# Second layer with the sample rows ahead of the prompt rows, and the last head's attention units in another order

## The chip, the cores and the metric

The kernel is one program on one NeuronCore of a Trainium2 chip. The core has five engines with instruction streams of their own, coupled by semaphores: TensorE (PE; the loading of its weights is listed as PEld), VectorE (DVE), ScalarE (ACT), GpSimd (POOL) and SyncE (SP, which here issues nearly all DMAs). Each engine works through its stream in the written order. The metric is the device time of one execution in microseconds; less is better. Three executions of the kernel before took 957.39 (median), 952.74 and 958.02 us.

## The reference

One inference step of a small hybrid decoder, for a prompt of 512 rows and for 8 x 4 = 32 sample rows that share all weights, with 1024 features:

```python
# layer 1: Mamba-2 mixer (32 heads of 64, state 128, causal convolution of width 4)
hp = hp + ssd_mixer(hp, ...);  hs = hs + ssd_mixer(hs, ...)
# shared keys and values, from the rows after layer 1
kv_p = rmsnorm(hp, kv_norm) @ w_kv;  kv_s = rmsnorm(hs, kv_norm) @ w_kv
# layer 2: three dilated windows per head (distances 0, d, .., 128 d with d = 1, 4, 16), 8 heads of 128
u = rmsnorm(h, g_norm) @ w_in          # 3 x 1024 columns of q, 1024 of the gate
o_g, lse_g = attend(q_g, bias_g)       # prompt: its own keys; samples: 1024 cached keys and the new ones
o = sum_g softmax_g(lse_g) * o_g
h = h + (o * silu(gate)) @ w_out
y = rmsnorm(h, final_norm)
```

Outputs are the normed rows, the Mamba states, the convolution's last rows and the new keys and values, each for prompt and samples.

## The kernel before

All activations lie transposed, features on the 128 partitions and the T = 544 rows along the free axis. Each fp32 operand of a large product is split into a high and a low fp32r part, and three matmuls (high x high, high x low, low x high) make one product. A row half of the second layer has TH = 272 columns.

**Stages.** From 0 to about 370 us the Mamba layer runs, then its output projection (`h1_tile`, which also puts the prompt rows into an order by residue mod 4), then keys and values (`v_out`, `k_out`), and from about 590 us the second layer. In the second layer the columns of every tile are the 512 prompt rows and then the 32 samples.

**The second layer** is a list `units` with work for one head each: `attend(h, n)` is query block n (128 rows) of the prompt for head h, `sample(h, q)` is four of the eight samples, and `combine()`, once, puts the samples' three windows together with a softmax over their logsumexps. At turn u a unit begins (scores on PE, softmax on DVE and ACT); at turns u+2, u+3 and u+4 it goes on (transposes `ptp` or `w`, the product with the values `pv` or `so`, a last transpose `op`). A head's `sample` fetches its cached keys `kc` (two tiles, two buffers) and values `vc` by DMA from SP.

**The filler.** After each turn, `run(24)` (from turn 44 on, `run(20)`) issues that many matmuls of a generator `filler()`: first 16 pairs of weight tiles for q and gate, each pair as 7 products of 12 matmuls over half the rows (`pa<-bq,whi`, `pb<-bq,wlo`, ...), then `out_proj`. The pairs' results are taken from PSUM by `q_evac` and `gate_evac`; in the last pair (gates of heads 4 and 6) the seven products come in the order 0, 1, 2, 3, 4, 6, 5, where 4 and 6 share one PSUM bank `pb`, so that 6 can start only after DVE has read what 4 left there. `out_proj` makes the output projection in two parts: first columns 272 to 543, then columns 0 to 271, 8 tiles of 24 matmuls each (`pa<-yh,wo`, `pa<-yl,wo`; the last two of each part read the weights from `whi` and `wlo`). Its operand is y = attention x gate, split into `yh` and `yl` by `y_split` (L1214 on ACT, L1215 on DVE) head by head, and for the samples by `sample_y`, which needs `combine`'s result `oc` and the samples' gates `u_s`.

**At the seam** between filler and output projection `combine` itself issues 16 filler matmuls between its 16 small matmuls `oc` (128 x 16); `ahead` takes these off an earlier turn. `combine` has two more transposes on PE: `lp` (the logsumexps) and, after a softmax in small steps on DVE and ACT (L1368 to L1385), `lp2` (its weights; a row of the profile shows both as `lp`). The second call of `sample_y` stands at the very end of the last pair.

**Order.** A framework turns this into one stream per engine; ACT, DVE and SP take their instructions strictly in it, so an instruction that waits holds all behind it. `tc.high_priority()` moves some evacuations forward.

Of the kernel before, what the change touches and what calls it, by code (L numbers as in the profile page):

```python
# [15 lines left out]
ALU = mybir.AluOpType  # L16
AX = mybir.AxisListType

D = 1024
SEQ = 512  # L20
NB = 8
TS = 4
T = SEQ + NB * TS
HA = 256
HB = T - HA
# [30 lines left out]
TH = T // 2  # L56
PE_ = SEQ - TH

# [66 lines left out]
def tile_yoco_step(  # L125
# [718 lines left out]
    def h1_tile(m, pa, pb):  # L844
        xk = wk.tile([128, T], F32, name="xk", bufs=2)
        dma(xk, xT[:, m, :])
        hm = h1[m // 4][:, m % 4, :]
        nc.vector.tensor_tensor(blk(hm[:, 0:HA], 2), perm(pa[:, 0:HA], 2), perm(rs_v[:, 0:HA], 2), op=ALU.mult)
        nc.vector.tensor_tensor(blk(hm[:, HA:SEQ], 2), perm(pb[:, 0:SEQ - HA], 2), perm(rs_v[:, HA:SEQ], 2), op=ALU.mult)
        nc.vector.tensor_tensor(hm[:, SEQ:T], pb[:, SEQ - HA:HB], rs_v[:, SEQ:T], op=ALU.mult)  # L850
        nc.vector.tensor_tensor(blk(hm[:, 0:SEQ], 4), blk(hm[:, 0:SEQ], 4), perm(xk[:, 0:SEQ], 4), op=ALU.add)
        nc.vector.tensor_tensor(hm[:, SEQ:T], hm[:, SEQ:T], xk[:, SEQ:T], op=ALU.add)
# [97 lines left out]
    def v_out(h, pa, pb):  # L950
        vt = wk.tile([128, T], F32, name="vt", tag="vt", bufs=2)
        nc.vector.tensor_tensor(vt[:, 0:HA], pa[:, 0:HA], rs_h[:, 0:HA], op=ALU.mult)
        nc.vector.tensor_tensor(vt[:, HA:T], pb[:, 0:HB], rs_h[:, HA:T], op=ALU.mult)
        dma(kvT[:, 8 + h, :], vt)
        yield
        vp = pss("vp", (128, 4, 128))
        vsp = pss("vsp")
        for n in range(4):
            transpose(vp[:, n, :], vt[:, 128 * n:128 * n + 128], ident)
        transpose(vsp[0:32, 0:128], vt[:, SEQ:T], ident)  # L960
# [116 lines left out]
    def q_evac(t, half_, p, other=None, sign=1.0):  # L1077
        h, g = t
        if t not in qp_t:
            qp_t[t] = wk.tile([128, SEQ], F32, name="qp", bufs=7)  # L1080
        n = PE_ if half_ else TH
        qs = qpad[h % 3][:, :, TS * g:TS * g + TS]
        for o, c0, c1 in ((qp_t[t][:, TH * half_:TH * half_ + n], 0, n), (qs, n, TH))[0:1 + half_]:
            src = p[:, c0:c1]
            if c0:
# [5 lines left out]
            nc.vector.scalar_tensor_tensor(o, src, sign * scale, samples(add) if c0 else add, op0=ALU.mult, op1=ALU.add)  # L1091

    def gate_evac(t, half_, p, other=None, sign=1.0):
# [8 lines left out]
        nc.scalar.activation(th, c, AF.Tanh, scale=0.5)  # L1102
        n = PE_ if half_ else TH
        yt = y_t[h // 4][:, h % 4, TH * half_:TH * half_ + n]
        u = yt if h == 7 else th[:, 0:n]
        nc.vector.scalar_tensor_tensor(u, th[:, 0:n], 1.0, c[:, 0:n], op0=ALU.add, op1=ALU.mult)
# [6 lines left out]
        nc.vector.scalar_tensor_tensor(yt, yt, 0.5, u, op0=ALU.mult, op1=ALU.mult)  # L1113
        y_split(h, TH * half_, TH * half_ + n)

# [125 lines left out]
    def attend(h, n):  # L1241
# [3 lines left out]
        vb, vr = (kv[:, i, 0:SEQ].rearrange("p (n d) -> p n d", n=4) for i in (1, 2))  # L1245
        ktr = kt[:, 0:SEQ].rearrange("p (n r i) -> p r n i", n=4, r=4)
        bt12 = bt[:, 256:512].rearrange("p (a c) -> p a c", a=2)
# [8 lines left out]
        mm(sp[:, 0:g0], qp[0][:, 128 * n:128 * n + 128], kt[:, k0:128 * n + 128], start=True, stop=True)  # L1256
        s_ = wk.tile([128, 512], F32, name="s", bufs=3)
# [36 lines left out]
        yt = y_t[h // 4][:, h % 4, :]  # L1294
        if h == 7 and op_n[h] % 2 == 0:
            c0 = HA if n > 1 else 0
            assert len(gated) == 2
            nc.vector.scalar_tensor_tensor(yt[:, c0:c0 + HA], op[:, c0:c0 + HA], 0.5, yt[:, c0:c0 + HA], op0=ALU.mult, op1=ALU.mult)
            y_split(h, c0, c0 + HA)
        elif h < 7 and op_n[h] == 4:  # L1300
            nc.vector.tensor_copy(yt[:, 0:SEQ], op)
            att_done.add(h)
# [5 lines left out]
    def sample(h, q):  # L1308
# [10 lines left out]
        for o, c0, c1 in ((s1, 0, 512), (s2, 512, NU), (s2, NU, SK)):  # L1319
            for j in range(4):  # L1320
                b = 4 * q + j
                keys = kc[j // 2][:, j % 2, c0:c1] if c1 <= NU else kt[:, SEQ + TS * b:SEQ + TS * b + TS]
                mm(o[32 * j:32 * j + 32, c0 % 512:c0 % 512 + c1 - c0], qs[:, b, :], keys, start=True, stop=True)
# [79 lines left out]
    def sample_y():  # L1403
        if len(late_smp) == 1:
            nc.vector.scalar_tensor_tensor(y_s, y_s, 0.5, u_s, op0=ALU.mult, op1=ALU.mult)
# [166 lines left out]
def _unpack(r):  # L1572
    yt = r["yT"].transpose(2, 1, 0).reshape(T, D)
    inv = np.arange(SEQ).reshape(4, 32, 4).transpose(0, 2, 1).reshape(-1)
    yp = np.empty((SEQ, D), np.float32)
    yp[inv] = yt[:SEQ]
    kv = r["kvT"].transpose(2, 1, 0).reshape(T, 2, ATH, 128)
    kvp = np.empty((SEQ, 2, ATH, 128), np.float32)
    kvp[inv] = kv[:SEQ]
    cv = r["convT"].transpose(2, 1, 0).reshape(27, CONV)  # L1580
# [3 lines left out]
        yp.reshape(1, SEQ, D),  # L1584
        np.ascontiguousarray(yt[SEQ:]).reshape(NB, TS, D),
        np.ascontiguousarray(sp).reshape(1, 1, NH, HP, NST),
# [3 lines left out]
        kvp.reshape(1, SEQ, 2, ATH, 128),  # L1590
        np.ascontiguousarray(kv[SEQ:]).reshape(NB, TS, 2, ATH, 128),
    )
# [13 lines left out]
```

## Time and profile before

| | us |
|---|---|
| three executions | 957.39, 952.74, 958.02 |
| the profiled execution | 955.35 |
| its span, first to last instruction | 953.6 |
| PE busy in the span | 924.2 (97%) |
| DVE / ACT / POOL busy | 685.5 / 477.6 / 201.9 |
| mean granted clock of TensorE | 0.983 |

The profiled execution's time is its span and 1.75 us around it. A page of the profile has each engine's busy time, the chain of waits that ended last, and the costliest groups of instructions. A row such as `L143 MATMUL pa<-bq,whi` is named by line, operation, output and inputs; nearly all matmuls share L143, since one helper issues them, and are told apart by their tiles. The trace adds, for each engine and stretch of time, the single instructions, what ended an engine's idle time, and the clock that TensorE was granted.

### The profile page before, as it was taken

To read this page: it belongs to the slowest core of one execution; us is meant where nothing else is said; L and a number is where in the kernel's file an instruction comes from. 1 tells how busy PE (TensorE), PEld (TensorE's weight loads), DVE (VectorE), ACT (ScalarE), POOL (GpSimd) and SP (SyncE) were. 2 spreads that over 40 slices of the span, in tenths; PEclk is the share of its full clock that TensorE was granted. 3 is DMA by queue.
4 is the path that set the end of the run, shared out by engine and by line. 5 is a ranking of instruction groups with operands and counts; after the bars stand their busy time and mean duration, and the time that the engine had idled before them with its cause. 6 is when DMAs were issued, how large, how long until landed. Compare 5 with 4: busy or idle time off the path is not lost.

```text
span 953.6 us, 21793 instructions
## 1 busy us (share of the span) xinstructions
PE 924.2 (97%) x8645; PEld 850.3 (89%) x8645; DVE 685.5 (72%) x1435; ACT 477.6 (50%) x1057; POOL 201.9 (21%) x295
## 2 busy tenths in 40 slices
PE   7999999899999998999999999999999999999896
PEld 5999888888888888999999999988888888879896
DVE  5688998998999888555488446866667767758532
ACT  5557754755655654322254213555545555566442
POOL 3232544734634732101101000000000000000121
PEclk9999999899999999999999999999999999999898
DMA  7252355254465433536286555766877767855311
GB/s 253 91 138 93 100 200 187 84 191 151 153 206 174 172 113 111 155 101 216 97 275 215 186 176 182 261 217 214 271 236 251 258 236 215 292 194 193 113 47 48
DMA packets 75934, 168.49 MB, mean 177 GB/s; under 512 B 19446, under 2 KB 37192, under 8 KB 75320
## 3 DMA queue, kind: packets, MB, share of 16 engines
q1 hardware_dynamic: 71880, 154.91, 49.5%
q10 hardware_dynamic: 2880, 9.44, 2.5%
q0 software_dynamic: 1072, 2.74, 1.1%
q8 instruction: 68, 1.11, 0.5%
q14 instruction: 34, 0.28, 0.1%
HBM read 141.14 MB, written 25.93 MB: 175 GB/s over the span
## 4 chain that ended last, share of the span: by engine, by line
PE 87%; DVE 6%; DMA 3%; ACT 1%; POOL 1%; issue 1%; SPq 0%; DVEq 0%; ACTq 0%
PE pa L143 34%; PE pb L143 30%; PE sp L143 3%; PE so L143 3%; PE pv L143 2%; PE s L143 2%; DMA kc<-ck 1%; PE yd L143 1%; PE csp L143 1%; PE yo L143 1%; PE ptp L146 1%; PE xp L146 1%; PE w L146 1%; DVE co L529 1%; PE yos L143 1%
## 5 line engine op out<-in xcount | busy, mean ns | idle before, releaser
L199 ACT ACTIVATE whi<-wraw 128x1024 fp32r<-128x1024 f32 x72 | 76.1, 1056 | 101.5 <-PE pb L143 68.9
L200 DVE TENSOR_TENSOR wlo<-wraw,whi 128x1024 fp32r<-128x1024 f32 x71 | 90.0, 1268 | 48.1 <-ACT whi L199 47.9
L143 PE MATMUL pa<-bq,whi 128*128 128x272 f32 x512 | 103.2, 297 | 0.0
L143 PE MATMUL pa<-xh,whi 128*128 128x256 f32 (+1 forms) x320 | 92.9, 294 | 3.3 <-ACT xh L365 3.3
L143 PE MATMUL pb<-xh,whi 128*128 128x288 f32 (+1 forms) x304 | 90.4, 299 | 3.9 <-ACT cb L331 3.9
L143 PE MATMUL pb<-xl,whi 128*128 128x288 f32 (+1 forms) x304 | 91.2, 302 | 0.9 <-DVE xl L368 0.8
L143 PE MATMUL pa<-xl,whi 128*128 128x256 f32 (+1 forms) x320 | 90.7, 287 | 1.1 <-DVE xl L368 1.1
L143 PE MATMUL pb<-xh,wlo 128*128 128x288 f32 (+1 forms) x304 | 87.4, 299 | 0.0
L143 PE MATMUL pa<-xh,wlo 128*128 128x256 f32 (+1 forms) x320 | 85.0, 283 | 0.0
L143 PEld LDWEIGHTS pa<-bq,whi 128*128 128x128 f32 x512 | 81.9, 190 | 0.9
L143 PE MATMUL pb<-bq,whi 128*128 128x272 f32 x384 | 78.4, 298 | 1.0 <-DVE qpad L1091 0.7
L143 PE MATMUL pa<-bq,wlo 128*128 128x272 f32 x256 | 74.3, 290 | 0.0
L529 DVE SCALAR_TENSOR_TENSOR co<-cb,cvp,co 128x568 f32<-128x568 f32 x72 | 66.1, 919 | 1.1 <-ACT co L527 0.2
L143 PEld LDWEIGHTS pa<-xh,whi 128*128 128x128 f32 x320 | 60.8, 190 | 6.4 <-ACT xh L365 4.0
L143 PEld LDWEIGHTS pa<-xl,whi 128*128 128x128 f32 x320 | 60.6, 189 | 3.5 <-DVE xl L368 1.6
L143 PEld LDWEIGHTS pb<-xl,whi 128*128 128x128 f32 x304 | 57.8, 190 | 6.4 <-issue 4.4
L143 PEld LDWEIGHTS pb<-bq,whi 128*128 128x128 f32 x384 | 61.4, 190 | 2.3 <-DVE qpad L1091 1.4
L143 PEld LDWEIGHTS pb<-xh,whi 128*128 128x128 f32 x304 | 58.0, 191 | 5.0 <-ACT cb L331 4.1
L1333 POOL COPY lse<-mxs 128x1 f32<-128x1 f32 x16 | 4.1, 258 | 265.5 <-DVE mxs L1331 265.5
L143 PEld LDWEIGHTS pa<-xh,wlo 128*128 128x128 f32 x320 | 58.0, 188 | 1.3 <-issue 0.9
L143 PEld LDWEIGHTS pb<-xh,wlo 128*128 128x128 f32 x304 | 56.6, 190 | 2.2 <-issue 2.2
L1158 ACT ACTIVATE whi<-wraw 128x512 fp32r<-128x512 f32 x64 | 40.1, 626 | 35.9 <-PE pb L143 14.8
(378 smaller groups left out, 2788.0 us busy)
## 6 DMA issues: line engine op xcount, KB each, us to landing
wraw<-w_in SPq DMA_DIRECT2D x40, 512.0 KB
kc<-ck SPq DMA_DIRECT2D x32, 640.0 KB
vc<-cv SPq DMA_DIRECT2D x32, 640.0 KB
wraw<-wb SPq DMA_DIRECT2D x32, 512.0 KB
s<-s SPq DMA_DIRECT2D x16, 512.0 KB
m<-aed SPq DMA_DIRECT2D x16, 512.0 KB
ssmS<-s ACTq DMA_DIRECT2D x16, 512.0 KB
wraw<-w_out SPq DMA_DIRECT2D x16, 512.0 KB
```

The source lines that it names most:

```text
L143: pin(nc.tensor.matmul(*a, **k))
L146: pin(nc.tensor.transpose(*a))
L199: a = nc.scalar.activation(hi, raw, AF.Copy)
L200: b = lo_eng.tensor_tensor(lo, raw, f32(hi), op=ALU.subtract)
L529: nc.vector.scalar_tensor_tensor(o, cb[:, k:k + n], cvp[:, ti, k:k + 1], o, op0=ALU.mult, op1=ALU.add)
L1158: nc.scalar.activation(hi, src[p][j], AF.Copy)
L1333: nc.gpsimd.tensor_copy(lse[:, i16:i16 + 1], mx[:, 2:3])
```

## The change

Three edits go together.

1. In the second layer the columns become 32 samples, then 512 prompt rows (NS = 32). `h1_tile` writes them so, and all readers (`v_out`, `q_evac`, `gate_evac`, `attend`, `sample`, `sample_y`, the outputs) follow. The output projection still does columns 272 to 543 first; these are now prompt rows 240 to 511 and no samples. The samples are in the part projected second.
2. The last head's units come in the order 1, 2, 3, 0 where they were 2, 3, 0, 1, so that blocks 1 to 3, of which the first part now needs rows, are done first. `sample(7, 1)`, `attend(7, 3)` and `combine` thereby stand one turn later. The product of attention and gate for head 7 is taken as 384 rows and 128 rows, where it was 256 and 256.
3. `ahead` is set one turn later, with `combine`.

```diff
@@ h1_tile
+        hp, hs_ = hm[:, NS:T], hm[:, 0:NS]
...
+        nc.vector.tensor_tensor(hs_, pb[:, SEQ - HA:HB], rs_v[:, SEQ:T], op=ALU.mult)
+        nc.vector.tensor_tensor(blk(hp, 4), blk(hp, 4), perm(xk[:, 0:SEQ], 4), op=ALU.add)
@@ q_evac
-        n = PE_ if half_ else TH
+        n = 0 if half_ else NS
         qs = qpad[h % 3][:, :, TS * g:TS * g + TS]
-        for o, c0, c1 in ((qp_t[t][:, TH * half_:TH * half_ + n], 0, n), (qs, n, TH))[0:1 + half_]:
+        d = TH * half_ - NS
+        for o, c0, c1 in ((qp_t[t][:, n + d:TH + d], n, TH), (qs, 0, n))[0:2 - half_]:
@@ gate_evac
+        n = 0 if half_ else NS
+        c0, c1 = TH * half_ + n, TH * half_ + TH
...
-        if half_:
-            nc.vector.scalar_tensor_tensor(u_s[:, h, :], th[:, n:TH], 1.0, c[:, n:TH], op0=ALU.add, op1=ALU.mult)
+        if n:
+            nc.vector.scalar_tensor_tensor(u_s[:, h, :], th[:, 0:n], 1.0, c[:, 0:n], op0=ALU.add, op1=ALU.mult)
@@ attend, its last step
-        if h == 7 and op_n[h] % 2 == 0:
-            c0 = HA if n > 1 else 0
+        if h == 7 and op_n[h] >= 3:
+            c0, c1 = ((128, SEQ), (0, 128))[op_n[h] - 3]
+            y7 = yt[:, NS + c0:NS + c1]
             assert len(gated) == 2
...
+            y_split(h, NS + c0, NS + c1)
@@ sample_y
-                split2(y_h[i][:, :, SEQ:T], y_l[i][:, :, SEQ:T], y_s[:, 4 * i:4 * i + 4, :])
+                split2(y_h[i][:, :, 0:NS], y_l[i][:, :, 0:NS], y_s[:, 4 * i:4 * i + 4, :])
@@ the units and their turns
-    units += [(sample, (7, 0)), (attend, (7, 2)), (sample, (7, 1)), (attend, (7, 3)), (combine, ()), (attend, (7, 0)), (attend, (7, 1))]
+    units += [(sample, (7, 0)), (attend, (7, 1)), (attend, (7, 2)), (sample, (7, 1)), (attend, (7, 3)), (combine, ()), (attend, (7, 0))]
...
-        if u == len(units) - 3 + SKIP:
+        if u == len(units) - 2 + SKIP:
             ahead[0] = ATH * OCN
```

**What moves on PE, at the turn where `sample(7, 1)` began.** Rows in the order of the stream; `s<-kc` are the samples' scores against the cached keys, `sp` the prompt's scores, `so` and `pv` products with values, `pa`/`pb<-bq` the filler. Before:

```order
L143 MATMUL pv<-kv,pt 32x128 x4
L143 MATMUL s_10992<-kc,qpad_6994 32x512 x4
L143 MATMUL s_10993<-kc,qpad_6994 32x128 x4
L143 MATMUL s_10993<-kv,qpad_6994 32x4 x4
L143 MATMUL pb<-bq_6880,whi 128x272 x2
```

And now, first the same place, then the next turn:

```order
L143 MATMUL pv<-kv,pt 32x128 x4
L143 MATMUL sp<-kv,qp 32x96 x8
L143 MATMUL sp<-kv,qp 128x256
L143 MATMUL pb<-bq_6880,whi 128x272 x2
...
L143 MATMUL so<-vn,wt 32x128 x4
L143 MATMUL s_11080<-kc,qpad_6994 32x512 x4
L143 MATMUL s_11081<-kc,qpad_6994 32x128 x4
L143 MATMUL s_11081<-kv,qpad_6994 32x4 x4
L143 MATMUL pa<-bq_6881,wlo 128x272
```

The scores of the last samples are behind 20 more filler matmuls, a prompt block's scores and the products `so` of the samples before them. The DMAs stand on SP as before, but for one fetch of weights that passed one of `h2`.

**On PE at the seam**, the last rows of the filler and the first of the output projection. Before:

```order
L143 MATMUL oc<-sbt,os 128x16 x2
L143 MATMUL pb<-bq_6882,wlo 128x272
...
L143 MATMUL pa<-bq_6881,whi 128x272 x2
L143 MATMUL pa<-bq_6881,wlo 128x272
L146 MATMUL ptp<-ident,s 128x128 x2
L146 MATMUL ptp<-ident,s 64x128
L143 MATMUL pv<-kv,pt 128x128
L143 MATMUL pv<-kv,pt 32x128 x4
L143 MATMUL pa<-yh,wo 128x272
L143 MATMUL pa<-yl,wo 128x272
```

And now:

```order
L143 MATMUL pb<-bq_6880,wlo 128x272
L143 MATMUL pb<-bq_6882,whi 128x272 x2
...
L143 MATMUL pa<-bq_6881,whi 128x272
L143 MATMUL oc<-sbt,os 128x16 x2
L143 MATMUL pa<-bq_6881,whi 128x272
L143 MATMUL pa<-bq_6881,wlo 128x272
L143 MATMUL pa<-yh,wo 128x272
L143 MATMUL pa<-yl,wo 128x272
```

The `oc` matmuls now end two filler matmuls ahead of the output projection, where 22 and a block's transposes and `pv` stood between; product 6 (`bq_6882`) follows product 4 (`bq_6880`) with no `oc` between them.

**On DVE, around `combine`'s softmax** (`qpad<-lp` is its first step, the last row of each piece its last; `yl<-y` are splits of y). Before:

```order
L1368 COPY qpad_6993<-lp 16x128
L1106 SCALAR_TENSOR_TENSOR y_6986<-kv 128x240
...
L1379 TENSOR_TENSOR qpad_6993<-qpad_6993 16x4x4 x3
L1215 TENSOR_TENSOR yl<-y_6985,yh 128x272
L1215 TENSOR_TENSOR yl<-y_6985,yh 128x240
L1159 TENSOR_TENSOR wlo<-wraw,whi 128x512
...
L1159 TENSOR_TENSOR wlo<-sums,whi 128x512
L1384 TENSOR_TENSOR qpad_6993<-qpad_6993 16x4x4 x3
```

And now, from a little ahead of it:

```order
L1163 TENSOR_TENSOR wlo<-sums,whi 128x512
...
L1219 TENSOR_TENSOR yl<-y_6985,yh 128x240
L1219 TENSOR_TENSOR yl<-y_6985,yh 128x272
L1374 COPY qpad_6993<-lp 16x128
L1219 TENSOR_TENSOR yl<-y_6986,yh 128x272
...
L1110 SCALAR_TENSOR_TENSOR kv<-kv,pa 128x240
...
L1388 RECIPROCAL qpad_6993<-qpad_6993 16x16
L1390 TENSOR_TENSOR qpad_6993<-qpad_6993 16x4x4 x3
```

All eight splits of heads 0 to 3 (`y_6985`), of which two stood within the softmax and six behind it, now stand ahead of its first step, five of them in a row just ahead. Within it now stand two splits of later heads (`y_6986`) and three operations of a gate, where it was two splits and two operations.

More of the change, by code (lines that the diff above doesn't have):

```diff
@@ L22 @@
 TS = 4
+NS = NB * TS
 T = SEQ + NB * TS
@@ L847, in h1_tile @@
         hm = h1[m // 4][:, m % 4, :]
[L848 to L852, printed above, removed]
+        hp, hs_ = hm[:, NS:T], hm[:, 0:NS]
+        nc.vector.tensor_tensor(blk(hp[:, 0:HA], 2), perm(pa[:, 0:HA], 2), perm(rs_v[:, 0:HA], 2), op=ALU.mult)
+        nc.vector.tensor_tensor(blk(hp[:, HA:SEQ], 2), perm(pb[:, 0:SEQ - HA], 2), perm(rs_v[:, HA:SEQ], 2), op=ALU.mult)
+        nc.vector.tensor_tensor(hs_, pb[:, SEQ - HA:HB], rs_v[:, SEQ:T], op=ALU.mult)
+        nc.vector.tensor_tensor(blk(hp, 4), blk(hp, 4), perm(xk[:, 0:SEQ], 4), op=ALU.add)
+        nc.vector.tensor_tensor(hs_, hs_, xk[:, SEQ:T], op=ALU.add)
         hh, hl = h_h[m // 4][:, m % 4, :], h_l[m // 4][:, m % 4, :]
@@ L958, in v_out @@
         for n in range(4):
-            transpose(vp[:, n, :], vt[:, 128 * n:128 * n + 128], ident)
-        transpose(vsp[0:32, 0:128], vt[:, SEQ:T], ident)
+            transpose(vp[:, n, :], vt[:, NS + 128 * n:NS + 128 * n + 128], ident)
+        transpose(vsp[0:32, 0:128], vt[:, 0:NS], ident)
         vb = wk.tile([128, 4, 128], F32, name="vb", tag="xk", bufs=2)
@@ L1090, in q_evac @@
             add = other[:, c0:c1]
-            nc.vector.scalar_tensor_tensor(o, src, sign * scale, samples(add) if c0 else add, op0=ALU.mult, op1=ALU.add)
+            nc.vector.scalar_tensor_tensor(o, src, sign * scale, samples(add) if smp else add, op0=ALU.mult, op1=ALU.add)
     def gate_evac(t, half_, p, other=None, sign=1.0):
@@ L1102, in gate_evac @@
         nc.scalar.activation(th, c, AF.Tanh, scale=0.5)
[L1103 to L1106, printed above, removed]
-        if half_:
-            nc.vector.scalar_tensor_tensor(u_s[:, h, :], th[:, n:TH], 1.0, c[:, n:TH], op0=ALU.add, op1=ALU.mult)
+        n = 0 if half_ else NS
+        c0, c1 = TH * half_ + n, TH * half_ + TH
+        yt = y_t[h // 4][:, h % 4, c0:c1]
+        u = yt if h == 7 else th[:, n:TH]
+        nc.vector.scalar_tensor_tensor(u, th[:, n:TH], 1.0, c[:, n:TH], op0=ALU.add, op1=ALU.mult)
+        if n:
+            nc.vector.scalar_tensor_tensor(u_s[:, h, :], th[:, 0:n], 1.0, c[:, 0:n], op0=ALU.add, op1=ALU.mult)
         if h == 7:
@@ L1321, in sample @@
                 b = 4 * q + j
-                keys = kc[j // 2][:, j % 2, c0:c1] if c1 <= NU else kt[:, SEQ + TS * b:SEQ + TS * b + TS]
+                keys = kc[j // 2][:, j % 2, c0:c1] if c1 <= NU else kt[:, TS * b:TS * b + TS]
                 mm(o[32 * j:32 * j + 32, c0 % 512:c0 % 512 + c1 - c0], qs[:, b, :], keys, start=True, stop=True)
@@ L1575, in _unpack @@
     yp = np.empty((SEQ, D), np.float32)
-    yp[inv] = yt[:SEQ]
+    yp[inv] = yt[NS:]
     kv = r["kvT"].transpose(2, 1, 0).reshape(T, 2, ATH, 128)
     kvp = np.empty((SEQ, 2, ATH, 128), np.float32)
-    kvp[inv] = kv[:SEQ]
+    kvp[inv] = kv[NS:]
     cv = r["convT"].transpose(2, 1, 0).reshape(27, CONV)
```

20 lines of the change are left out of this document (10 added, 10 removed).

## The prediction

> **What bounds the kernel now.** I read the page's busy shares first, then the waits of TensorE over the second layer's end, then the single instructions around the two longest of them, then the granted clock.
>
> ```profile
> span 953.6 us, 21793 instructions
> PE 924.2 (97%) x8645; PEld 850.3 (89%) x8645; DVE 685.5 (72%) x1435; ACT 477.6 (50%) x1057; POOL 201.9 (21%) x295
> ```
>
> PE is busy for 97% of the span, so a change that leaves the matmuls alone can only win what PE waits, or what it loses at a lower clock. These are the waits from 780 us on that touch the places where the change reorders PE:
>
> ```profile
> PE pa L143 <- ACT yh L1214: 2.5, 1, 2.5
> PE s L143 <- DMA kc<-ck: 1.9, 1, 1.9
> PE pb L143 <- DVE kv L1100: 0.2, 1, 0.2
> ```
>
> The first is the seam: the output projection's first matmul waits for a split of y. The seam, engine by engine, PE first, then ACT, then DVE:
>
> ```profile
> 884.67 0.29 PE L143 MATMUL pa<-bq,wlo 128*128 128x272 f32 x1
> 884.80 0.49 PE L146 MATMUL ptp<-ident,s 128*128 128x128 f32 x3
> 885.12 0.74 PE L143 MATMUL pv<-kv,pt 128*128 128x128 f32 x10
> 888.33 0.59 PE L143 MATMUL pa<-yh,wo 128*128 128x272 f32 x1 [2.46 <-ACT yh L1214]
> 885.32 0.37 ACT L1276 COPY pt<-ptp 128x256 f32<-128x256 f32 x1 [3.02 <-PE ptp L146]
> 887.98 0.49 ACT L1214 ACTIVATE yh<-ys 128x128 fp32r<-128x128 f32 x2
> 887.47 0.41 DVE L1405 SCALAR_TENSOR_TENSOR ys<-ys,us 128x256 f32<-128x256 f32 x1
> ```
>
> What came last was `yh<-ys`, the samples. ACT had stood idle for 3.02 us ahead of it: the copy `pt` of the block that was then last but one waited for PE's transposes, and all gates' work queued behind it. Behind the seam the matmuls then run without a gap, in the chain of waits as one piece:
>
> ```profile
> 897.67 22.14 PE pa L143 x176
> ```
>
> A step of the filler or of the output projection is thus 22.14/176 = 0.126 us. Now the clock, in equal stretches of 3.41 us (the clock is the column after the busy times, 1.00 is full):
>
> ```profile
> 877.19:880.60 3.41, 3.23 (x28) 3.13 (x28) 0.73 (x2) 1.06 (x1) 0.00 (x0) 1.00 0.99 374
> 880.60:884.02 3.42, 3.42 (x17) 3.42 (x17) 3.19 (x6) 1.64 (x3) 0.00 (x0) 0.51 0.77 246
> 884.02:887.43 3.41, 1.84 (x20) 1.45 (x19) 1.48 (x6) 1.60 (x6) 0.00 (x0) 0.99 0.60 217
> 887.43:890.84 3.41, 2.51 (x10) 2.32 (x11) 2.32 (x8) 1.47 (x5) 0.00 (x0) 0.51 0.00 0
> 890.84:894.26 3.42, 3.42 (x17) 3.42 (x16) 0.00 (x0) 0.00 (x0) 0.00 (x0) 0.50 0.00 0
> 894.26:897.67 3.41, 3.41 (x33) 3.04 (x32) 0.63 (x2) 1.97 (x4) 0.00 (x0) 0.99 0.01 2
> ```
>
> The clock was halved twice: from 880.60 for one stretch, after the one full of 16-column `oc` matmuls, and from 887.43 for two, after the one with the seam's wait. A full stretch holds 33 matmuls at full clock and 17 at half.
>
> **The change part by part.** *The seam's wait, removed: -2.46.* The part projected first has no samples now, so `yh<-ys` is out of its way. Late next would be the splits of heads 7, 6 and 4, whose rows it uses last. Behind the last filler matmul now come 15 matmuls of long finished heads, 15 x 0.126 = 1.9 us, then a `pv` of 0.74: 2.6 us. DVE then has, ahead of head 7's low split, the last gate's sum, another product and the split itself: about three operations of 0.4 us, 1.2 to 1.4 us. Head 4's needs another 1 us, and its matmuls come 0.9 us later. So a cover of about 1.3 us remains. The 384 columns that replace 256 add about 0.15 us to one of these. If that cover is gone, each late us costs a us.
>
> *The clock behind it: -2.97.* From 888.33 to 894.26 PE worked 5.93 us at half clock, which is 2.97 us at full. Without the wait I expect no halving there. The nearest row that speaks for the opposite is the other long wait, which left the clock as it was:
>
> ```profile
> 837.00:854.00 17.00, 14.96 (x186) 11.44 (x180) 10.14 (x29) 9.84 (x29) 0.18 (x1) 1.00 0.68 228
> 854.00:880.00 26.00, 25.82 (x329) 23.47 (x326) 19.59 (x76) 16.33 (x41) 0.18 (x1) 1.00 0.45 149
> ```
>
> A wait need not halve the clock, then, and a stretch of small matmuls can. Bounds: 0 and -2.97; I take the whole, as the halving starts at the first stretch border after the wait began. The half-clock stretch behind the `oc` matmuls I keep, because 16 `oc` and 16 filler matmuls still alternate; without it the result is 3.42/2 = 1.71 us lower.
>
> [...]
>
> *The samples' scores, one turn later: -1.89.* The wait for the cache and what SP did ahead of it:
>
> ```profile
> 850.14 1.03 PE L143 MATMUL s<-kc,qpad 128*32 128x512 f32 x4
> 853.06 0.62 PE L143 MATMUL s<-kc,qpad 128*32 128x512 f32 x6 [1.89 <-DMA kc<-ck]
> 844.44 0.80 SPq L1338 DMA_DIRECT2D vc<-cv  x2
> 845.97 0.33 SPq L1317 DMA_DIRECT2D kc<-ck  x1
> 845.97 7.05 DMA kc<-ck
> ```
>
> SP held the second `kc` behind `vc`, and that behind the preceding samples' `so`; none of these moves, so the tile still lands at 853.02. The scores now come behind a block's scores, 20 filler matmuls (2.5 us), transposes and `so`: even the 2.5 us alone puts them at 850.14 + 1.0 + 2.5 = 853.7. Bounds: 0, if the transfer is slower by more than 2 us, and -1.89. What else moved a turn is the same work later.
>
> *The softmax of `combine`: +0.8.* Its second transpose did not wait before:
>
> ```profile
> 864.20 0.28 PE L146 MATMUL lp<-ident,lse 128*16 128x128 f32 x1
> 870.10 0.23 PE L146 MATMUL lp<-ident,qpad 16*128 16x16 f32 x1
> 864.85 0.26 DVE L1368 COPY qpad<-lp 16x128 f32<-16x128 f32 x1
> 868.52 0.32 DVE L1384 TENSOR_TENSOR qpad<-qpad 16x16 f32<-16x16 f32 x3
> 868.77 2.08 DVE L1215 TENSOR_TENSOR yl<-y,yh 128x272 fp32r<-128x272 f32 x6
> 860.00:865.00 5.00, 5.00 (x47) 4.63 (x46) 4.72 (x17) 4.07 (x12) 0.00 (x0) 1.00 0.90 305
> 865.00:870.00 5.00, 5.00 (x90) 4.34 (x89) 4.95 (x22) 3.53 (x12) 0.00 (x0) 1.00 0.13 52
> ```
>
> From `lp` to the last step on DVE were 868.84 - 864.20 = 4.64 us; PE had 5.90 us of other work between the transposes and has as many matmuls now. DVE is full there (9.67 of 10 us), so what is put ahead of the chain delays it: five splits in a row (2.08/6 = 0.35 us each, 1.73) and a gate's operation (0.33) make 6.7 us, 0.8 over. Bounds: 0, if the splits ran before `lp`, and 8 x 0.35 + 0.33 + 4.64 - 5.90 = 1.9 with all eight. Behind the waiting transpose stand `pv` and the whole filler.
>
> *Product 6 right behind product 4: +0.35.*
>
> ```profile
> 878.89 0.29 PE L143 MATMUL pb<-bq,wlo 128*128 128x272 f32 x1
> 879.02 0.51 PE L143 MATMUL oc<-sbt,os 128*128 128x16 f32 x4
> 879.22 0.44 DVE L1100 SCALAR_TENSOR_TENSOR kv<-pb,sums 128x272 f32<-128x272 f32 x1 [2.28 <-PE pb L143]
> 879.72 0.52 PE L143 MATMUL pb<-bq,whi 128*128 128x272 f32 x2 [0.18 <-DVE kv L1100]
> ```
>
> DVE's read lies between 878.89 and 879.72, 0.83 us, of which four `oc` records fill 0.35. With nothing between, these 0.35 are lost. Bounds: 0.2 and 0.7, if DVE comes late.
>
> *The queries: -0.2.* In the first turns PE once waited for the second of two reads of that bank, the samples' (their column group is now with the half that ACT reads):
>
> ```profile
> PE pb L143 <- DVE qpad L1091: 0.7, 1, 0.7
> ```
>
> Product 4's result is read by one DVE operation now. Bounds 0 and -0.7; the read itself stays, so I take the lower third. The 12 small reads go to ACT, which is busy for 50%; they cost nothing as long as that holds, else some 0.2 us each.
>
> *At nothing:* the columns' new places (equal operations and sizes in `h1_tile`, `v_out`, `attend`; hidden or not, they take what they took); the samples' splits and the last block, now needed 8 tiles x 24 x 0.126 = 24 us later; the half of `h2` that is now fetched behind a tile of weights, needed 4 tiles, 12 us, into the first part.
>
> Sum: -2.46 - 2.97 - 1.89 + 0.8 + 0.35 - 0.2 = -6.4 us. The profiled execution took 955.35, which gives 949.0. It lay 2.0 us under the median of the three runs and 2.6 over the lowest; the mean of all four is 955.9, so I add 0.5: **949.5**.
>
> **The rivals.**
>
> *The clock stays low.* If not the wait halved the clock but little work in the array, the new `lp2` wait, the wait between products 4 and 6 and the `oc` matmuls, now close together, halve it again for as many stretches. For: the stretch from 877.19, busy 3.23 of 3.41 us, halved the clock, while 1.89 us of waiting at 851 did not. Against: the second halving starts right after the longest wait. 949.5 + 2.97 = 952.5. [...]
>
> *The seam's wait passes to the next splits.* DVE and ACT hold the splits of heads 7, 6 and 4 behind the casts of `wo` and the last gates. For: ACT was blocked for 3.02 us there. Against: the cover of 1.3 us, and that the blocking `pt` copy is no longer followed by what the first part needs. Seam and clock then give nothing: 949.5 + 2.46 + 2.97 = 954.9.
>
> *Slower: DVE falls behind at `combine`.* Its full stretch from 860 to 870 is asked for 1.9 us earlier. With all 16 splits (14 more than stood within) ahead of the chain's end, `lp2` waits 14 x 0.35 + 0.33 - 1.26 = 4.0 us, the clock is halved as after the seam (2.97), and the splits for the first output tile are as late as before (seam and its clock stay). 955.35 - 1.89 + 0.35 + 4.0 + 2.97 = 960.8. Slower by over 0.5% begins where that wait is over 3.3 us. Against: DVE idles shortly before, and can take splits up there:
>
> ```profile
> 858.08 0.17 DVE L1363 TENSOR_TENSOR lse<-lsm,lse 128x16 f32<-128x16 f32 x1 [1.10 <-ACT lsm L1362]
> 860.27 0.41 DVE L1106 SCALAR_TENSOR_TENSOR kv<-kv 128x240 f32<-128x240 f32 x1 [0.82 <-ACT kv L1102]
> ```
>
> **How the numbers follow.** Forecast 0.55, with 0.08 more for the case that the `oc` stretch keeps its clock too (947.8); low clock 0.20; seam's wait passed on 0.11; slower 0.06. About 0.5%, 4.8 us, is what a measurement can tell from no change (the three runs differ by 0.55%). Against some 956 us the border lies at 951.1: all of the 0.08, six sevenths of the forecast and a quarter of the low-clock case lie beyond it, 0.60; slower 0.06; the rest 0.34. The range reaches down to 945 (947.8 less the bounds of +0.8, -0.2 and the runs' scatter) and up to 956, which takes in the passed-on wait.
>
> **What would show it.** Right: no wait of PE for `yh` or for `kc` behind 845 us, a clock of 1.00 from the first `pa<-yh,wo` on (or one half stretch behind `oc`), a wait of 0 to 2 us for `qpad` L1390, one of about 0.5 us for `kv` L1103. Wrong: a wait at the 16th to 24th matmul of the first output tile, two or more half-clock stretches between 870 and 895, or a new wait before 780 us.

## The result, and the profile after

The changed kernel takes 947.26 us (median of 5 runs, 946.21 to 949.58) where the kernel before takes 956.19 (median of 5, 952.74 to 958.02): a ratio of 0.9912, 95% interval 0.9884 to 0.9941. Two more comparisons, made with the experiments, gave 0.9925 (0.9896 to 0.9953) and 0.9901 (0.9864 to 0.9938). Over all runs the mean is 947.6 us (17 runs) against 956.4 (62 runs): 8.8 us. The forecast was 949.5 with a range of 945 to 956.

The profiled execution after took 946.21 us, with a span of 944.4 and a clock of 0.991 (before: 0.983). The busy shares of its page:

```profile
span 944.4 us, 21805 instructions
PE 916.7 (97%) x8645; PEld 844.0 (89%) x8645; DVE 682.1 (72%) x1423; ACT 478.7 (51%) x1069; POOL 200.5 (21%) x295
```

Of PE's waits from 780 us on (us in total, times, longest), those at the places that the change touches:

```profile
PE lp L146 <- DVE qpad L1390: 0.7, 1, 0.7
PE pb L143 <- DVE kv L1103: 0.5, 1, 0.5
PE s L143 <- DMA kc<-ck: 0.4, 1, 0.4
```

The count of matmuls is the same. The waits of 2.5 us for `yh` and of 1.9 for `kc` are gone; the `kc` wait of 0.4 belongs to the sample unit ahead. Two small waits stand in their place, both foreseen. The seam and the samples' scores, instruction by instruction (PE alone), with the last transpose `op` ahead of the scores, in the timeline of single instructions:

```profile
842.48 0.27 PE L146 MATMUL op<-ident,on 128*128 128x128 f32 x1
855.51 1.28 PE L143 MATMUL s<-kc,qpad 128*32 128x512 f32 x16
856.61 0.22 PE L143 MATMUL s<-kv,qpad 128*32 128x4 f32 x8
872.54 0.20 PE L146 MATMUL lp<-ident,qpad 16*128 16x16 f32 x1 [0.69 <-DVE qpad L1390]
875.97 0.52 PE L143 MATMUL pb<-bq,whi 128*128 128x272 f32 x2 [0.53 <-DVE kv L1103]
882.86 0.29 PE L143 MATMUL pa<-bq,wlo 128*128 128x272 f32 x1
882.99 0.29 PE L143 MATMUL pa<-yh,wo 128*128 128x272 f32 x1
```

The output projection's first matmul follows the filler's last within 0.13 us, one step: the seam holds nothing up. The scores of the samples are one block of 1.28 us. In the chain of waits, the piece behind the seam now starts here:

```profile
889.02 22.14 PE pa L143 x176
```

Over the whole stretch between, the clock (the column behind the busy times) stays full:

```profile
842.48:889.02 46.54, 45.32 (x552) 40.46 (x551) 34.79 (x114) 30.41 (x79) 0.64 (x1) 1.00 0.53 183
```

The same place before, from `op` to the piece of 176 matmuls, reads

```profile
842.59 0.27 PE L146 MATMUL op<-ident,on 128*128 128x128 f32 x1
```

and 897.67 (shown with the prediction): 55.08 us against 46.54. This distance is the yardstick below, because it holds every place that the change touches at the end of the second layer, and none of the chance that lies ahead.

### The profile page after: what moved, and what is told of

It is laid out like the page before. It is cut to its first block, busy times and chain, and to the rows that moved or that the text cites. A ratio compares the mean times of both kernels' runs of the same rounds, so it can differ in the third digit from the quotient of the medians.

```text
span 944.4 us, 21805 instructions
## 1 busy us (share of the span) xinstructions
PE 916.7 (97%) x8645; PEld 844.0 (89%) x8645; DVE 682.1 (72%) x1423; ACT 478.7 (51%) x1069; POOL 200.5 (21%) x295
## 4 chain that ended last, share of the span: by engine, by line
PE 85%; DVE 6%; DMA 5%; ACT 2%; POOL 1%; issue 1%; DVEq 0%; SPq 0%; ACTq 0%
PE pa L143 34%; PE pb L143 29%; PE sp L143 3%; PE pv L143 2%; PE so L143 2%; PE s L143 2%; DMA m<-aed 2%; DMA kc<-ck 1%; PE yd L143 1%; PE csp L143 1%; PE w L146 1%; PE ptp L146 1%; PE yo L143 1%; PE xp L146 1%; PE yos L143 1%
```

## The experiments

All times stand beside runs of the kernel before on the same chip; "distance" is that from the last `op` before the samples' scores to the piece of 176 matmuls, in us of the profiled execution.

| Run | PE waits for y | samples' scores, us | half clock, 845 to 900 us | distance | median us (runs) |
|---|---|---|---|---|---|
| before, 1st profile | 2.46 | 4.2 | 3.42 and 6.83 | 55.08 | 956.19 (5) |
| before, 2nd | 2.47 | 4.3 | none | 51.12 | |
| before, 3rd | 2.47 | 4.6 | 6.83 | 54.03 | |
| after, 1st | none | 1.3 | none | 46.54 | 947.26 (5) |
| after, 2nd | none | 1.3 | none | 46.57 | 947.67 (6) |
| after, 3rd | none | 1.3 | none | 46.58 | 946.05 (6) |
| units alone | 2.00 + 0.31 | 1.3 | 6.83 | 52.00 | 954.46 (12) |
| sample unit back | none | 4.6 | 3.41 | 50.22 | 949.85 (9) |
| head 4 first | 1.66 | 1.3 | 6.83 | 51.47 | 951.25 (12) |
| head 4 third | 0.91 + 0.2 | 1.3 | none | 48.18 | 949.68 (12) |
| plain order | 0.75 | 1.3 | none | 47.10 | 946.98 (6) |
| eight splits on GpSimd | none | 1.3 | none | 47.06 | 949.17 (8) |
| the same, and product 5 cut | none | 1.3 | none | 46.58 | 948.57 (7) |
| four splits on GpSimd, product 5 cut | none | 1.3 | none | 45.32 | 944.48 (6) |

Timed together were the second run of after with "units alone", "sample unit back" and "head 4 first"; "head 4 third" with "plain order" and the two with eight splits; and the last with the third run of after. Beside the group of "head 4 third" the changed kernel was not timed, so its runs are set against after by way of before.

**The changed kernel again.** No edit.

> The changed kernel again, as the measure for the others. Theory: every term of the prediction holds, about 9 us (1%) less than before, no half-clock stretch between 842 and 935 us, waits of 0.7 us for `qpad` L1390 and 0.5 us for `kv` L1103. Rival (the half-clock stretches fall by chance from one execution to the next): this profile has one or two of 3.4 us between 870 and 895 us again, and the time of this execution is 1.7 to 3.4 us longer than that of the first profile of it.

It took 0.9925 of before, with the same two waits and a distance within 0.03 us of the first. The half-clock stretches ahead of 400 us moved (one at 247 us and one at 377 us were not there in the first profile), so the rival is right for those: they come and go. Behind 842 us none came.

**The units' order alone.** The rows stay prompt, samples; everything else is as after. (What the text below calls the pairs' order, 4, 6, 5 in the last pair, is no difference: the kernel before has it too.)

```
-        if h == 7 and op_n[h] % 2 == 0:
-            c0 = HA if n > 1 else 0
+        if h == 7 and op_n[h] >= 3:
+            c0, c1 = ((128, SEQ), (0, 128))[op_n[h] - 3]
...
-    units += [(sample, (7, 0)), (attend, (7, 2)), (sample, (7, 1)), (attend, (7, 3)), (combine, ()), (attend, (7, 0)), (attend, (7, 1))]
+    units += [(sample, (7, 0)), (attend, (7, 1)), (attend, (7, 2)), (sample, (7, 1)), (attend, (7, 3)), (combine, ()), (attend, (7, 0))]
...
-        if u == len(units) - 3 + SKIP:
+        if u == len(units) - 2 + SKIP:
```

> The units' order and the pairs' order alone; the rows stay prompt, samples. Theory (the seam's wait and the clock behind it belong to the rows' order): PE's wait for `kc` is gone and the samples' scores take about 1.3 us in place of 4.2, so about 2.9 less; waits for `qpad` L1390 (about 0.7) and `kv` L1103 (about 0.5) appear as in the changed kernel; but the first output tile waits 2 to 3 us for `yh<-ys` again, with a half-clock stretch or two behind it (1.7 to 3.4 us). So about 2 us less than before in all, and 6 to 7 us more than the changed kernel. Rival (the rows' order is worth nothing, the turn of the units removed the seam's wait too): no wait for `yh`, and within 1 us of the changed kernel.

The ratio to before was 0.9979 (0.9960 to 0.9997), 2.1 us, and 6.8 us more than the changed kernel in the same comparison. The scores come in 1.3 us, and the seam waits for the samples' split again, with the clock behind it at half for two stretches. First the single instructions of PE, then the stretches of 3.41 us from the one with the wait on:

```profile
885.02 0.57 PE L143 MATMUL pa<-yh,wo 128*128 128x272 f32 x1 [2.00 <-ACT yh L1214]
885.90 0.60 PE L143 MATMUL pa<-yl,wo 128*128 128x272 f32 x1 [0.31 <-DVE yl L1215]
```

```profile
881.65:885.07 3.42, 1.43 (x13) 1.21 (x12) 2.31 (x7) 1.51 (x5) 0.00 (x0) 1.00 0.42 159
885.07:888.48 3.41, 3.10 (x12) 2.79 (x13) 1.42 (x5) 0.53 (x2) 0.00 (x0) 0.50 0.00 0
888.48:891.89 3.41, 3.41 (x21) 2.80 (x20) 0.00 (x0) 0.23 (x1) 0.00 (x0) 0.50 0.00 0
```

So the seam's gain needs the new rows, and the scores' gain comes with the units alone. The rows' order alone was not tried: with the old units the split of block 1 would come behind the matmuls that read it.

**The last sample unit back at its old turn.**

```
-    units += [(sample, (7, 0)), (attend, (7, 1)), (attend, (7, 2)), (sample, (7, 1)), (attend, (7, 3)), (combine, ()), (attend, (7, 0))]
+    units += [(sample, (7, 0)), (attend, (7, 1)), (sample, (7, 1)), (attend, (7, 2)), (attend, (7, 3)), (combine, ()), (attend, (7, 0))]
```

> The changed kernel with the last sample unit of head 7 back at its old turn, right behind the block 1. Theory: PE waits 1.5 to 1.9 us for `kc` again and the samples' scores take about 4.2 us in place of 1.3: 2 to 2.9 us slower than the changed kernel, with no wait for `yh`. Rival (the transfer was hidden anyway by the new rows; the gain came from the seam alone): no wait for `kc` over 0.5 us, within 0.5 us of the changed kernel.

The wait is back, and the run is 2.2 us above the changed kernel; by the distance it is 3.7. (The wait of 0.7 us for `qpad` L1390 is not there in this run.) The scores in PE's timeline, and the stretches around them:

```profile
851.08 1.03 PE L143 MATMUL s<-kc,qpad 128*32 128x512 f32 x4
854.09 0.62 PE L143 MATMUL s<-kc,qpad 128*32 128x512 f32 x6 [1.99 <-DMA kc<-ck]
```

```profile
851.55:854.97 3.42, 1.43 (x16) 0.49 (x14) 0.64 (x4) 2.65 (x9) 0.00 (x0) 1.00 0.57 234
854.97:858.38 3.41, 3.41 (x22) 3.34 (x19) 1.29 (x6) 1.77 (x3) 0.18 (x1) 0.50 0.01 2
```

The first rows also suggest why the wait of 1.99 us costs about 3: with one cache tile there, 4 matmuls of scores, all of 512 columns, take 1.03 us, while in the changed kernel, with both there, 16 take 1.28 (8 of 512 columns and 8 of 128, merged in one row). Of four, two read the one tile and two the other (`kc[j // 2]`). In the changed kernel's first profile the first four start within 0.03 us from 855.51 on and the next four from 855.96; in the first profile of before, with one tile there, two start at 850.14 and the next two at 850.57. A round of two thus took as long as a round of four, 0.43 us against 0.45, and with the tiles apart there are twice as many. That this is the cause is my estimate from these starts; no run takes it apart. Here the clock was halved behind this wait as well, which none of the three profiles of the kernel before shows.

**Head 4 first in the first output tile.** The same matmuls, but the head that is split last is needed first, so that the changed kernel gets a wait at its seam.

```
-                yield from proj_steps(p, [wos[m]], y_h, y_l, c0, c1, order=(0, 1, 2, 3, 5, 7, 6, 4))
+                yield from proj_steps(p, [wos[m]], y_h, y_l, c0, c1, order=(4, 0, 1, 2, 3, 5, 7, 6) if part == 0 and m == 0 else (0, 1, 2, 3, 5, 7, 6, 4))
```

> The changed kernel, with the first output tile's heads in the order 4, 0, 1, 2, 3, 5, 7, 6 in place of 0, 1, 2, 3, 5, 7, 6, 4: the same matmuls, but the head that is split last is needed first, so that the seam gets a wait again that the change did not have. Theory (a wait of about 2 us at the seam halves the clock behind it, as in the kernel before): a wait of 1.5 to 2.5 us for a split of y ahead of the first output tile, a half-clock stretch or two of 3.4 us behind it, and 3.2 to 5.9 us over the changed kernel. [...] Rival 2 (the splits are ready, there is a cover of more than 2 us): no wait, no difference.

A wait of 1.66 us, and 3.6 us more than the changed kernel; by the distance 4.9, which is about the wait of 1.66 and half of the 6.35 us from its end (887.94) to the end of the half clock (894.29). The stretches from the one with the wait on:

```profile
884.04:887.45 3.41, 2.24 (x20) 2.02 (x18) 2.25 (x6) 0.89 (x3) 0.00 (x0) 1.00 0.49 162
887.45:890.87 3.42, 2.93 (x11) 2.64 (x12) 2.45 (x9) 1.28 (x5) 0.00 (x0) 0.50 0.00 0
890.87:894.28 3.41, 3.41 (x22) 2.80 (x20) 0.00 (x0) 0.00 (x0) 0.00 (x0) 0.50 0.00 0
```

**Head 4 third.** Needed six matmuls later than in the run before it.

```
-                yield from proj_steps(p, [wos[m]], y_h, y_l, c0, c1, order=(0, 1, 2, 3, 5, 7, 6, 4))
+                yield from proj_steps(p, [wos[m]], y_h, y_l, c0, c1, order=(0, 1, 4, 2, 3, 5, 7, 6) if part == 0 and m == 0 else (0, 1, 2, 3, 5, 7, 6, 4))
```

> The changed kernel with the first output tile's heads in the order 0, 1, 4, 2, 3, 5, 7, 6: head 4, split last, is needed 6 matmuls or 0.75 us later than in the run with head 4 first, which waited 1.7 us and then lost 6.83 us to half clock (3.4 us). Theory (the clock is halved by how little work a stretch of 3.41 us holds): a wait of 0.7 to 1.2 us, clock 1.00 behind it, 0.7 to 1.2 us more than the changed kernel, so that 0.75 us of wait less saves about 2.5 to 4 us against that run. Rival (any wait ahead of the first output tile halves the clock): wait 0.7 to 1.2 us and one or two half-clock stretches, 2.4 to 4.6 us more than the changed kernel.

The wait was 0.91 us, with 0.2 for a second split, and the clock stayed full:

```profile
885.42:888.83 3.41, 2.46 (x20) 2.13 (x21) 2.73 (x9) 1.56 (x5) 0.00 (x0) 1.00 0.05 18
888.83:892.25 3.42, 3.42 (x34) 3.22 (x34) 0.85 (x2) 2.19 (x4) 0.00 (x0) 1.00 0.00 0
```

The distance is 3.3 us shorter than with head 4 first, for 0.75 us of wait less. So it is not any wait that halves the clock. (By the medians, taken in different comparisons, only 1.6 us; the ratios to before, 0.9928 with 0.9900 to 0.9956 here and 0.9954 with 0.9934 to 0.9975 there, overlap.)

**The plain order of the last pair's products.** 4, 5, 6 in place of 4, 6, 5. This order is no part of the change, and not new as the expectation has it: the kernels before and after both have 4, 6, 5.

```
-            return p, (0, 1, 2, 3, 4, 6, 5)[j] if p == len(pairs) - 1 else j
+            return p, j
```

> The changed kernel with the last pair's products in the plain order 4, 5, 6 in place of 4, 6, 5. Theory (the wait for `kv` L1103 is the price of the new order, and buys head 4's split an earlier place): that wait, 0.5 us, is gone, but the first output tile waits for a late split of y, 0.8 to 1.7 us; so 0.3 to 1.2 us more than the changed kernel (0.03 to 0.13%), and no half clock behind it, since less than 1.9 us of a stretch of 3.41 stand idle. Rival 1 (the order buys nothing): no wait for y, 0.5 us less than the changed kernel. Rival 2 (any wait at the seam halves the clock): the same wait, with one or two half-clock stretches behind it, 2 to 4.6 us more than the changed kernel.

The wait for `kv` is gone, the first output tile waits 0.75 us for head 4's split, no half clock follows, and the distance is 0.5 us longer. The time, 0.9897 of before (0.9859 to 0.9935), can't be told from the changed kernel's. So the order 4, 6, 5 is worth half a microsecond to the changed kernel by the profile, and nothing that the runs' times can show. The reason that the expectation gave for the clock, under 1.9 us of a stretch idle, fits the run with the units alone (half clock behind a stretch with 1.99 us idle, at 881.65, and none behind one with 1.78, at 373.07) but does not hold by itself: with head 4 first PE was busy for 2.24 us of the stretch ahead of the half clock, so that it followed 1.17 us of idling.

**The kernel before, twice more.** No edit; one profile each.

> The kernel before, for a second profile of it. Theory (the seam's wait halves the clock in every execution; the stretch behind the `oc` matmuls is halved only if the 3.41 us stretches happen to lie so): a wait for `yh` of about 2.5 us with 6.83 us of half clock behind it again; a half-clock stretch at 880 us in one or neither of this profile and the next. Rival (both belong to the program): the half-clock stretches at 880 and 887 us stand in both profiles as in the first.

> The kernel before, for a third profile of it; what is expected is told with the second.

Neither half-clock piece stands in all three profiles, so neither belongs to the program; the theory had the seam's halving in every execution, and that was wrong too. The wait at the seam is 2.47 us in both. In the second profile of before the clock stayed full behind it; in the third it was halved for 6.83 us. The stretch with the wait and the next, of the second and then of the third:

```profile
884.73:888.14 3.41, 1.84 (x21) 1.45 (x19) 3.02 (x10) 1.59 (x6) 0.00 (x0) 1.00 0.81 232
888.14:891.55 3.41, 2.42 (x17) 2.21 (x18) 2.33 (x8) 1.47 (x5) 0.00 (x0) 1.00 0.19 79
```

```profile
885.92:889.33 3.41, 1.53 (x19) 1.14 (x17) 3.02 (x11) 1.90 (x7) 0.00 (x0) 1.00 0.83 241
889.33:892.74 3.41, 2.82 (x11) 2.62 (x12) 2.02 (x7) 1.17 (x4) 0.00 (x0) 0.50 0.13 52
```

The borders of the stretches lie elsewhere against the work in each execution. In the second profile the stretch with the wait was followed by one in which PE idled for another microsecond, so the waiting was shared out; in the third more of it lay in one stretch (PE was busy for 1.53 us there, against 1.84). The `oc` matmuls were followed by half clock in neither, so I was right to leave that open and wrong to keep it in the sum.

**The changed kernel a third time.**

> The changed kernel again, as the measure for the run with two heads' splits on GpSimd. About 1% less than before; no half clock between 842 and 935 us; waits of 0.7 us for `qpad` L1390 and 0.5 us for `kv` L1103.

0.9901 of before, distance 46.58, the same two waits.

**Eight low splits on GpSimd.**

```
-        split2(y_h[i][:, k, c0:c1], y_l[i][:, k, c0:c1], y_t[i][:, k, c0:c1])
+        dh, dl, src = y_h[i][:, k, c0:c1], y_l[i][:, k, c0:c1], y_t[i][:, k, c0:c1]
+        nc.scalar.activation(dh, src, AF.Copy)
+        (nc.vector if i else nc.gpsimd).tensor_tensor(dl, src, f32(dh), op=ALU.subtract)
```

> The changed kernel with the low splits of heads 0 to 3 (eight subtractions of 128 rows by 272 or 240, 0.35 us each on DVE) on GpSimd, which has next to nothing to do from 858 to 893 us and takes about 0.85 us for such an operation. Theory (`combine` waits because five of these splits stand ahead of its softmax on DVE): the wait for `qpad` L1390, 0.7 us, is gone, that for `kv` L1103 stays near 0.5; 0.7 us less than the changed kernel, no wait for `yl`, since eight splits take about 7 us on GpSimd and are needed 10 us after `lp`. Rival 1 (the casts of the weights and the gates hold the softmax): the wait stays above 0.4 us, no difference. Rival 2 (GpSimd is too slow): a new wait of PE for `yl` in the first output tile, up to 2 us more.

The wait did not go, it grew to 1.05 us, and that for `kv` L1103 from 0.53 to 0.69. Neither theory nor rival 1 had the reason, which stands on GpSimd and then on DVE:

```profile
864.65 6.53 POOL L1230 TENSOR_TENSOR yl<-y,yh 128x240 fp32r<-128x240 f32 x8 [4.17 <-PE pa L143]
871.21 0.44 DVE L1230 TENSOR_TENSOR yl<-y,yh 128x272 fp32r<-128x272 f32 x1 [1.97 <-POOL yl L1230]
871.57 0.27 DVE L1376 COPY qpad<-lp 16x128 f32<-16x128 f32 x1
```

The low tile of heads 4 to 7 takes the space of y of heads 0 to 3, so its first split, on DVE, must wait for the last of the eight on GpSimd; `combine`'s copy stands behind it. DVE was not full, it stood still for 1.97 us.

**The same, and product 5 cut.** Four matmuls of product 5 are drawn ahead of product 6, the rest follows it.

```
-            return p, (0, 1, 2, 3, 4, 6, 5)[j] if p == len(pairs) - 1 else j
+            return p, j
...
-                yield from product(b, j, o, j not in (2, 6), True)
+                prod = product(b, j, o, j not in (2, 6), True)
+                if last and j == 5:
+                    rest = prod, o
+                    for _ in range(4):
+                        next(prod)
+                        yield
+                    continue
+                yield from prod
...
+                if last and j == 6:
+                    yield from rest[0]
...
```

> The run with the splits on GpSimd, and besides four matmuls of product 5 drawn ahead of product 6 (0.5 us of other work while DVE reads product 4's bank; the other eight follow product 6). Theory (both waits are the change's price and can be hidden): `qpad` L1390 gone, `kv` L1103 at 0.0 to 0.2 us; 1.1 to 1.2 us (0.12%) less than the changed kernel. Rival (head 4's split comes 0.5 us later and is late for the first output tile): a wait for `yh` or `yl` there of up to 0.7 us, so that 0.5 to 0.7 us remain.

The wait for `kv` fell from 0.53 to 0.19 us without a new one at the seam; that for `qpad` stayed at 1.07. Together no gain: the distance is the changed kernel's.

**Four low splits on GpSimd**, those of heads 0 and 1, with product 5 cut; the edit against the run before it.

```
-        (nc.vector if i else nc.gpsimd).tensor_tensor(dl, src, f32(dh), op=ALU.subtract)
+        (nc.vector if h > 1 else nc.gpsimd).tensor_tensor(dl, src, f32(dh), op=ALU.subtract)
```

> The run with both waits covered, but only the low splits of heads 0 and 1 on GpSimd (four, about 3.3 us), those of heads 2 and 3 on DVE. With all eight on GpSimd the softmax of `combine` did not get ahead: DVE stood 1.97 us for the first low split of heads 4 to 7, whose tile takes the place of y of heads 0 to 3, so that it had to wait for GpSimd's last split at 871.2 us, and the copy of `lp` stood behind it. Theory (the softmax is late by what stands ahead of it on DVE, splits and what they wait for): GpSimd ends at about 868 us, DVE has two or three splits fewer ahead of `lp`'s copy than in the changed kernel, the wait for `qpad` L1390 falls from 0.7 to 0.0 to 0.3 us, that for `kv` L1103 from 0.5 to 0.2; 0.7 to 1.0 us (0.1%) less than the changed kernel. Rival (what holds the softmax is the casts and gates, whoever makes the splits): the wait stays at 0.6 us or more, no difference beyond 0.3 us.

Both waits are gone. GpSimd is done before the first low split of heads 4 to 7 is due, at 866.18 us, and `combine`'s copy follows `lp` by 2.06 us (863.90 to 865.96) where it took 3.07 in the changed kernel:

```profile
861.06 3.82 POOL L1241 TENSOR_TENSOR yl<-y,yh 128x240 fp32r<-128x240 f32 x4 [4.18 <-PE pa L143]
863.90 0.28 PE L146 MATMUL lp<-ident,lse 128*16 128x128 f32 x1
865.96 0.27 DVE L1387 COPY qpad<-lp 16x128 f32<-16x128 f32 x1
869.82 0.23 PE L146 MATMUL lp<-ident,qpad 16*128 16x16 f32 x1
```

The distance is 45.32 us, 1.25 less than after. The time is 944.48 us, 0.9885 of before (0.9847 to 0.9924), where the changed kernel in the same comparison had 946.05 and 0.9901: the fastest of all, though a step of 0.1% or 0.2% is more than these runs can prove; the profile carries it. The 1.25 us are a little more than the 0.7 to 1.0 expected.

## Why the prediction was right, step by step

The direction, the range and the mechanism of the large terms held: the seam's wait and the wait for the cache went, and the two small waits came where they were foreseen. One case was weighed wrongly, the stretch behind `oc`, and three sizes were off. The time lies 2.2 us under the forecast; the terms account for it.

**The seam's wait, -2.46: right.** It stood at 2.46 to 2.47 us in three profiles of before and is gone in every kernel with the new rows. A wait for another split (0.75 to 1.66 us) came there only where the order of the heads or of the last products was changed. The cover that I put at 1.3 us can be tried against the runs in which head 4 comes sooner: wanted at once its split is 1.66 us late, and in the changed kernel's order its matmuls come 21 steps later, 21 x 0.126 = 2.6 us, with a `pv` of 0.7 between. That leaves 1.7 us, if the split comes at the same time in both; the splits did not become late, as the second rival had it. (Between the matmuls of heads 7 and 4 lie six steps, 0.76 us and not the 0.9 that I took, which changes nothing here.)

**The clock behind it, -2.97: the cause right, the size that of one execution.** From the end of the seam's wait on, the three profiles of before ran 5.93, 0 and 6.25 us at half clock (the third from 889.92 to 896.17), of which half is lost: 3.0, 0 and 3.1, 2.0 on average. That the full -2.97 fitted the first profile is chance. I read one profile as if its half-clock stretch were part of the program. The bounds of 0 and -2.97 that I gave were both real; I should have taken a value between them. The rival that the clock stays low lost: nothing between 842 and 935 us was halved in three profiles of the changed kernel, with the two new waits and the `oc` matmuls in place.

**The stretch behind `oc`, kept: wrong.** I gave the case that it keeps its clock a chance of 0.08, because the 16 + 16 matmuls still alternate. In the 13 other profiles, two of them of the kernel before, it was not halved once. It was the rare case that I had taken for the rule. In the first profile of before that stretch held PE's wait of 0.18 us for `kv` L1100 (busy 3.23 of 3.41 us); in the second and third the wait fell into the next stretch. In the first pair of profiles it is worth 1.71 us.

**The samples' scores, -1.89: right in kind, too small.** They now take 1.3 us in place of 4.2, 4.3 and 4.6: -2.9 to -3.3. I took the wait from the list; but the matmuls around such a wait are slow too (4 in 1.03 us against 16 in 1.28). I put that down to their starting two at a time with one tile there and four at a time with both, an estimate from the starts in the first profiles of before (850.14, 850.57) and after (855.51, 855.96) that no run takes apart.

**The softmax of `combine`, +0.8: right.** A wait of 0.69 to 0.70 us; from `lp`, which begins at 865.87 us, to the second transpose at 872.54 are 6.67 us against 5.90, +0.77. On DVE five low splits stood ahead of the copy, as worked out:

```profile
867.26 1.76 DVE L1219 TENSOR_TENSOR yl<-y,yh 128x272 fp32r<-128x272 f32 x5
868.94 0.27 DVE L1374 COPY qpad<-lp 16x128 f32<-16x128 f32 x1
```

The run with four of the splits on GpSimd took the wait away. The slower rival needed this wait over 3.3 us.

**Product 6 behind product 4, +0.35: right.** 0.53 us against 0.18.

**The queries, -0.2: too small.** From the first matmul of product 0 to `op`, the four profiles with the old rows take 262.3 to 263.7 us (mean 262.9), the ten with the new ones 260.5 to 262.1 (mean 261.3): 1.6 us. The wait for `qpad` L1091 (0.7, 0.5, none and 0.9 us with the old rows, never with the new) is a third of it; the waits for `kc` are shorter by some 0.2 us on average (0.8 to 0.6). The rest, about half, is in no wait that the lists show, and stays open.

The sum by the averages of the profiles: the distance 53.41 (55.08, 51.12, 54.03) to 46.56 gives -6.85; the part ahead of it -1.6; together -8.4 of the measured -8.8. By the forecast's own terms: -1.0 to -1.4 more from the scores, -1.4 more from the queries, -0.6 more from the stretch behind `oc` (1.71 in one profile of three), 0.9 less from the clock behind the seam. What the prediction's text called wrong, a wait at the 16th to 24th matmul of the first output tile, two half-clock stretches, or a new wait ahead of 780 us, did not appear.

## What to carry to other kernels

Before half clock seen in one profile is booked as a gain, look at the work in the stretch of 3.41 us ahead of it, and take a second profile: such a loss is a chance, not a term (here 5.93, 0 and 6.25 us at half clock behind one and the same wait of 2.46 to 2.47 us). A wait behind a DMA can cost more than its idle time: here 1.9 us of waiting went with 2.9 us of delay, where the matmuls around it started two at a time in place of four. And when work is moved to an idle engine to clear a full one, look first at whose memory its result takes: a buffer that is handed on can turn idle help into a wait, here one of 1.97 us on DVE.

## What the runs showed of the hardware

**Half clock came in stretches of 3.41 us, behind stretches with little work.** In all 14 profiles the half-clock pieces start on a grid of 3.41 us, which lies differently against the program in each execution. (In the first profile of before they last one or two stretches of 3.413 us and start 45, 61, 148 and 2 such stretches after one another.) Counting from the trace's records the columns of the matmuls begun in a stretch (272 for a row of `128x272`; a full stretch has 27 of these, some 7300; the 33 in the prediction's row include shorter ones), over all stretches at full clock behind the first 20 us: with under 2500 columns, 38 of 38 were followed by half clock; between 2500 and 3250, 15 of 32; above, none of 3651. For the seam's stretch in the three profiles of before this reads 3024 (halved), 3296 (not), 2480 (halved); with head 4 first 1808 (halved), third 4576 (not); behind the `oc` matmuls 2976 in the first profile of before (halved), 2768 to 3792 in the others (not). The last figures show that the count does not sort the cases sharply. In the band from 2500 to 3250, the 11 stretches in which PE was busy throughout were none of them followed by half clock.

So neither the wait as such nor PE's busy time tells by itself: the `oc` stretch with 3.23 us busy was followed by half clock, that of head 4 third with 2.46 us was not. The columns come nearest, but no run changed them alone, so that they are the cause is inferred.

The same count goes with whether one stretch is lost or two. Of the stretches at half clock, those with under 2900 columns were all followed by another (15 of 15), between 2900 and 3250 4 of 9, above none of 34. The first halved stretch held 2720 to 2992 in the four cases of two behind the seam, and 4080 and 3792 in the two cases of one, behind `oc` and behind the wait for `kc`.

**DVE was slower while GpSimd worked.** While GpSimd's four splits ran (861.06 to 864.88 in the last run), two splits on DVE took 0.63 us each, where the prediction has 0.35, and a weight's low part took 1.25 us; afterwards the latter took 0.67:

```profile
860.98 1.26 DVE L1241 TENSOR_TENSOR yl<-y,yh 128x240 fp32r<-128x240 f32 x2
862.16 1.25 DVE L1163 TENSOR_TENSOR wlo<-wraw,whi 128x512 fp32r<-128x512 f32 x1
868.09 0.67 DVE L1163 TENSOR_TENSOR wlo<-sums,whi 128x512 fp32r<-128x512 f32 x1
```

In the run with eight splits on GpSimd a weight's low part took 0.82 and 0.84 us beside them. Work moved to GpSimd was thus not free for DVE here. Why, no run takes apart, and that GpSimd is slowed in turn was not measured.
